# Where the weights' parts stand inside their tiles: 23 products and 24 units of a feed-forward moved by multiples of 8 and 16 bytes

## The chip, the cores and the metric

The kernel runs on one core of one Trainium2 chip. The metric is the device time of one execution in microseconds. A profile shows one execution, engine by engine; TensorE is "PE", its weight loads are "PEld", VectorE is "DVE", ScalarE "ACT", GpSimd "POOL" and SyncE "SP".

## The reference

One layer of a bidirectional encoder over 256 tokens of width 2048, all in float32: an RMSNorm and a combined input projection; windowed grouped-query attention with 12 query and 4 key/value heads beside a Fourier group; an output projection with residual; then the feed-forward, which the change is about, and a last RMSNorm.

```python
def _conv_ffn(h, w_up, dw_w, dw_b, w_down):
    up = h @ w_up
    gate, val = up[..., :D_FF], up[..., D_FF:]
    gate = lax.conv_general_dilated(gate, dw_w, ...) + dw_b
    act = jax.nn.gelu(gate, approximate=False) * val
    return act @ w_down
...
        x = x + _conv_ffn(_rmsnorm(x, norm2_g), w_up, dw_w, dw_b, w_down)
    return _rmsnorm(x, normf_g)
```

D_FF is 5504, or 43 tiles of 128 features.

## The kernel before, in words

**Parts.** Every weight tile of 128 × 2048 is loaded as float32 and split into two float32r parts: ScalarE writes `hi` (a copy rounded to float32r), VectorE writes `lo = w − hi`. A product of two float32 matrices is then three matmuls of parts, hi·hi, hi·lo and lo·hi. `split` (line 157) does this for a unit, `split_product` (line 919) for a down product; both issue their next loads behind the split. `hi` and `lo` each rotate through three buffers of 2176 elements, of which 2048 are used, so a part may start up to 128 elements into its tile. The list `shifts` holds that start, in elements of 4 bytes, for each unit. Before the change it is (hi, lo) = (16, 16) for the first eight units, (0, 16) for the query and key units and for all gate and value units, and (0, 0) for the rest; the down products always take (0, 0). 16 elements are 64 bytes.

**Units.** A gate or value unit is the up-projection to one tile of 128 features. `still_weights` (lines 304 to 311) keeps the weights still: for each of the 16 slices of the width it loads 128 × 128 of `hi` and streams the tokens' two parts past it (512 columns, line 308), then loads 128 × 128 of `lo` and streams the tokens' first part (256 columns, line 309): 32 matmuls in one bank of PSUM. The query and key units of the attention have the same form. `moving_weights` (lines 292 to 302) is the other form, used by the first projections, the output projection and the late part of the down-projection: activations stand still and 512 columns of weights stream past.

**Products.** The down-projection of the first 32 feature tiles is done group by group (four groups of eight tiles). In each group, for each half of the columns (c = 0, 1), seven products of sums of blocks stand for eight block products. `by_parts` (lines 1034 to 1040) does one: for each of four slices a piece of the operand is loaded as weights, and 512 columns of the product's `hi` (lines 1038 and 1039) or `lo` (line 1040) are streamed: 12 matmuls.

**Order.** The order of the work is written out by hand. `ff_items` (line 69) lists the feed-forward: 16 units, then for each group the pattern `"uuu" + "su" * 13 + "s"`, where u is a unit of the next group and s a product of this one, then what is left over. While item n is on TensorE, `ff_step` (line 960) issues the split of item n + 2 to ScalarE and VectorE, beside the post-processing of the items behind. All loads of weights go through SP's queue or, for the two sums that a DMA accumulates, through POOL's.

Of the kernel before, what the change touches and what calls it, by code (L numbers as in the profile page):

```python
# [9 lines left out]
F32R = mybir.dt.float32r  # L10
# [3 lines left out]
P = 128  # L14
# [20 lines left out]
SHIFT = 16  # L35
# [15 lines left out]
for _g in range(NKV):  # L51
# [10 lines left out]
PRODUCTS = [  # L62
    ["P1", "P7", "N5", "N3", "P6", "P2", "N4"], ["P1", "N5", "P7", "N3", "P6", "P2", "N4"]
]
# [4 lines left out]
def ff_items():  # L69


    def ups(tiles):
        return [(kind, j) for j in tiles for kind in ("gate", "val")]

    items = ups(range(8))
    for g in range(N_GROUPS):
        todo = {
            "u": ups(range(8 * g + 8, 8 * g + 16)),
            "s": [("product", g, c, p) for c in range(2) for p in PRODUCTS[c]],
        }  # L80
        items += [todo[c].pop(0) for c in PATTERN]
        assert not any(todo.values())
    items += [("down", 0, c) for c in range(4)] + ups(LAST)
    items += [("down", 1, c) for c in range(4)] + [("last", c) for c in range(4)]
    return items
# [3 lines left out]
def block_kernel(  # L89
# [22 lines left out]
    wp = ctx.enter_context(tc.tile_pool(name="wp", bufs=1))  # L112
# [3 lines left out]
    def f32(ap):  # L116
        return ap.bitcast(F32)
# [7 lines left out]
    shifts = [(SHIFT, SHIFT)] * 8 + [(0, SHIFT)] * 16 + [(0, 0)] * 16  # L125
    n_front = len(units)
    items, up_index = ff_items(), {}
    for n, it in enumerate(items):
        if it[0] == "product":
            continue  # L130
        up_index[n] = len(units)
        if it[0] in ("gate", "val"):
            units.append((w_up[2 * it[1] + (it[0] == "val")], 2048))
            shifts.append((0, SHIFT))
            continue
        elif it[0] == "down":
            units.append((w_down_late[4 * it[1] + it[2]], 2048))
        else:
            units.append((w_down_last[it[1]], 512 * len(LAST)))
        shifts.append((0, 0))  # L140
# [9 lines left out]
    def parts_of(i):  # L150
        halves[i] = tuple(
            wp.tile([P, 2176], F32R, tag=h, name=f"{h}{i}", bufs=3)[:, s : s + 2048]
            for h, s in zip(("hi", "lo"), shifts[i])
        )
        return halves[i]
# [44 lines left out]
    def u_part(k, o, n, m=1):  # L200

        rows = ux[k // 4][:, (k < 4) * U_HEAD :].rearrange("p (k c) -> p k c", k=4)
        return rows[:, k % 4 : k % 4 + m, o : o + n]
# [148 lines left out]
    for k in range(NK):  # L352
        c, q = k // 4, k % 4
        if q == 0:
            hi, lo = (t.rearrange("p (k c) -> p k c", k=4) for t in parts_of(c))
        n = 1 if c < 2 else 2
# [3 lines left out]
        if q % n == 0:  # L360
            w, h = u_part(k, 0, FW, n), hi[:, q : q + n, :]
# [545 lines left out]
    def weights_of(g, c, w):  # L907
        return w_down[(g * 2 + c) * 4 + "abcd".index(w)]

    def ring_load():  # L910
        if ring_next[0] < len(ring):
            key = ring[ring_next[0]]
            ring_next[0] += 1
            ring_tiles[key] = fp.tile([P, 2048], F32, tag="rawd", name="rawd%d%d%s" % key)
            nc.sync.dma_start(ring_tiles[key], weights_of(*key))
# [3 lines left out]
    def split_product(g, c, p):  # L919

        raw = {w: ring_tiles.get((g, c, w)) for w in "abcd"}
        x = ring_tiles["x"]
        src = {"P1": raw["a"], "N3": raw["d"], "P7": raw["b"], "P2": raw["c"]}.get(p, x)
        hi, lo = (
            wp.tile([P, 2176], F32R, tag=h, name=f"{h}_{p}_{g}{c}", bufs=3)[:, 0:2048]
            for h in ("hi", "lo")
        )
        halves["product", g, c, p] = (hi, lo)
        nc.scalar.activation(hi, src, AF.Copy)  # L929
        nc.vector.tensor_tensor(lo, src, f32(hi), ALU.subtract)  # L930
        if p in ("P1", "P7", "N3", "P2"):
            ring_load()
        elif p == "N5":
            nc.gpsimd.dma_start(x, weights_of(g, c, "d"), accum_op=ALU.add)
        elif p == "P6":
            nc.gpsimd.dma_start(x, weights_of(g, c, "c"), accum_op=ALU.add)
        elif p == "N4" and (g, c) != (N_GROUPS - 1, 1):
            pending.append(lambda: first_sums(g + c, 1 - c))

    def first_sums(g, c):  # L940

        a, b = ring_tiles[g, c, "a"], ring_tiles[g, c, "b"]
        x = ring_tiles["x"] = fp.tile([P, 2048], F32, tag="sumw", name=f"sumw{g}{c}", bufs=1)
        nc.vector.tensor_tensor(x, a, b, ALU.add)
        nc.gpsimd.dma_start(b, weights_of(g, c, "d"), accum_op=ALU.add)

    def split_item(n):
        if n >= len(items):
            return
        it = items[n]  # L950
        if n in up_index:
            split(up_index[n])
            if pending:
                pending.pop(0)()
        else:
            while pending:
                pending.pop(0)()
            split_product(*it[1:])
# [159 lines left out]
    for n, it in enumerate(items):  # L1118
# [15 lines left out]
        if it[0] == "product":  # L1134
            kind, g, c, p = it
# [10 lines left out]
        else:  # L1146
            kind, g, c = it
            hi, lo = halves.pop(up_index[n])
# [161 lines left out]
```

## Time and profile before

| | |
|---|---|
| median of 3 runs | 952.45 us (951.67 to 953.35) |
| the profiled execution | 951.68 us |
| its span, first to last instruction | 949.9 us |
| granted TensorE clock | 0.997 of full speed |
| TensorE busy | 940.3 us, 99% of the span, 5085 matmuls |
| VectorE, ScalarE busy | 750.6 us (79%), 534.5 us (56%) |
| mean DMA traffic | 223 GB/s |

A row of a group reads: line, engine, operation, out<-in, shapes, count, then busy time in us, mean ns of one, idle time before. The matmuls are pipelined and the profile models their ends, so two neighbours overlap in it: the distance between their starts is what they cost, and a mean over the undisturbed mean shows that something was lost. A row of the order of time begins with the start and the duration in us.

### The profile page before, as it was taken

To read this page: it belongs to the slowest core of one execution; us is meant where nothing else is said; L and a number is where in the kernel's file an instruction comes from. 1 tells how busy PE (TensorE), PEld (TensorE's weight loads), DVE (VectorE), ACT (ScalarE), POOL (GpSimd) and SP (SyncE) were. 2 spreads that over 40 slices of the span, in tenths; PEclk is the share of its full clock that TensorE was granted. 3 is DMA by queue.
4 is the path that set the end of the run, shared out by engine and by line. 5 is a ranking of instruction groups with operands and counts; after the bars stand their busy time and mean duration, and the time that the engine had idled before them with its cause. 6 is when DMAs were issued, how large, how long until landed. Compare 5 with 4: busy or idle time off the path is not lost.

```text
span 949.9 us, 12779 instructions
## 1 busy us (share of the span) xinstructions
PE 940.3 (99%) x5085; PEld 813.4 (86%) x5085; DVE 750.6 (79%) x935; ACT 534.5 (56%) x646; POOL 43.4 (5%) x58
## 2 busy tenths in 40 slices
PE   9999999999999999999999999999999999999996
PEld 7889998888888888888888888888888888888885
DVE  7758877666676689787898978988779979888775
ACT  7756766455454546556565555665556755553442
POOL 0000000000000000000000000000000000000003
PEclk9999999999999999999999999999999999999998
DMA  9854444446556675978778787877977797776542
GB/s 363 336 187 144 168 142 169 139 172 221 178 177 227 257 224 192 292 234 262 228 257 248 237 304 228 264 250 214 296 253 239 210 296 218 221 244 218 179 134 89
DMA packets 32108, 211.58 MB, mean 223 GB/s; under 512 B 3504, under 2 KB 4016, under 8 KB 7984
## 3 DMA queue, kind: packets, MB, share of 16 engines
q1 hardware_dynamic: 28448, 184.55, 52.4%
q0 software_dynamic: 3600, 26.22, 14.6%
q8 instruction: 40, 0.66, 0.3%
q14 instruction: 20, 0.16, 0.0%
HBM read 208.65 MB, written 2.10 MB: 222 GB/s over the span
## 4 chain that ended last, share of the span: by engine, by line
PE 98%; DVE 1%; DMA 0%; issue 0%; ACT 0%; POOL 0%; POOLq 0%; DVEq 0%; ACTq 0%
PE ps_gate L308 16%; PE ps_val L308 16%; PE ps_gate L309 8%; PE ps_val L309 8%; PE ps_q L308 5%; PE ps_P L1039 3%; PE ps_P L1038 3%; PE ps_P L1040 3%; PE ps_q L309 2%; PE ps_N L1039 2%; PE ps_N L1038 2%; PE ps_a L300 2%; PE ps_a L298 2%; PE ps_N L1040 2%; PE ps_a L299 2%; PE ps_k L308 2%
## 5 line engine op out<-in xcount | busy, mean ns | idle before, releaser
L165 DVE TENSOR_TENSOR lo<-raw,hi 128x2048 fp32r<-128x2048 f32 (+1 forms) x133 | 302.7, 2276 | 54.0 <-ACT hi L164 54.0
L164 ACT ACTIVATE hi<-raw 128x2048 fp32r<-128x2048 f32 (+1 forms) x133 | 253.1, 1903 | 59.7 <-PE ps_l L299 24.7
L308 PE MATMUL ps_gate<-hU,hi 128*128 128x512 f32 x688 | 236.8, 389 | 0.0
L308 PE MATMUL ps_val<-hU,hi 128*128 128x512 f32 x688 | 236.8, 389 | 0.0
L309 PE MATMUL ps_gate<-hU,lo 128*128 128x256 f32 x688 | 190.2, 276 | 0.0
L309 PE MATMUL ps_val<-hU,lo 128*128 128x256 f32 x688 | 190.2, 276 | 0.0
L308 PEld LDWEIGHTS ps_gate<-hU,hi 128*128 128x128 f32 x688 | 129.1, 188 | 27.1
L308 PEld LDWEIGHTS ps_val<-hU,hi 128*128 128x128 f32 x688 | 129.1, 188 | 27.1
L309 PEld LDWEIGHTS ps_gate<-hU,lo 128*128 128x128 f32 x688 | 129.1, 188 | 1.1
L309 PEld LDWEIGHTS ps_val<-hU,lo 128*128 128x128 f32 x688 | 129.1, 188 | 1.1
L820 ACT ACTIVATE ft_g<-ps_gate 128x256 f32<-128x256 f32 x43 | 16.5, 384 | 121.1 <-PE ps_gate L309 121.1
L820 ACT ACTIVATE ft_v<-ps_val 128x256 f32<-128x256 f32 x43 | 16.5, 385 | 89.9 <-PE ps_val L309 89.9
L308 PE MATMUL ps_q<-hT,hi 128*128 128x512 f32 x192 | 66.9, 393 | 0.0
L309 PE MATMUL ps_q<-hT,lo 128*128 128x256 f32 x192 | 53.2, 277 | 0.0
L1039 PE MATMUL ps_P<-hi_P,op_P 128*128 128x512 f32 x128 | 50.2, 392 | 0.0
L1038 PE MATMUL ps_P<-hi_P,op_P 128*128 128x512 f32 x128 | 50.1, 392 | 0.0
L1040 PE MATMUL ps_P<-lo_P,op_P 128*128 128x512 f32 x128 | 49.8, 389 | 0.0
L930 DVE TENSOR_TENSOR lo_N<-sumw,hi_N 128x2048 fp32r<-128x2048 f32 x16 | 36.6, 2290 | 10.1 <-ACT hi_N L929 10.1
L308 PEld LDWEIGHTS ps_q<-hT,hi 128*128 128x128 f32 x192 | 36.1, 188 | 7.2
L822 DVE TENSOR_TENSOR fa_g<-ps_gate,ft_g 128x256 f32<-128x256 f32 x43 | 18.2, 423 | 25.0 <-ACT ft_g L820 25.0
L298 PE MATMUL ps_a<-hi,cat 128*128 128x512 f32 x96 | 37.9, 395 | 0.0
L1039 PE MATMUL ps_N<-hi_N,op_N 128*128 128x512 f32 x96 | 37.6, 392 | 0.0
(332 smaller groups left out, 1608.1 us busy)
## 6 DMA issues: line engine op xcount, KB each, us to landing
raw<-in_w_up SPq DMA_DIRECT2D x86, 1024.0 KB, 5.1
raw<-in_w_in SPq DMA_DIRECT2D x20, 1024.0 KB, 4.9
raw<-in_w_out SPq DMA_DIRECT2D x16, 1024.0 KB, 4.8
sumw<-in_w_down POOLq DMA_DIRECT2D x16, 1024.0 KB, 8.5
raw<-in_w_down_late SPq DMA_DIRECT2D x8, 1024.0 KB, 4.8
raw<-in_w_down_last SPq DMA_DIRECT2D x4, 768.0 KB, 4.3
ux<-in_w_u_x SPq DMA_DIRECT2D x3, 768.0 KB, 9.5
xs<-in_x SPq DMA_DIRECT2D x4, 512.0 KB, 16.2
```

The costliest lines, as they stand in the source:

```text
L164: nc.scalar.activation(hi[:, 0:n], raw[:, 0:n], AF.Copy)
L165: nc.vector.tensor_tensor(lo[:, 0:n], raw[:, 0:n], f32(hi[:, 0:n]), ALU.subtract)
L298: nc.tensor.matmul(ps, ah, wh, start=first and q == q0, stop=False)
L299: nc.tensor.matmul(ps, al, wh, start=False, stop=False)
L300: nc.tensor.matmul(ps, ah, wl, start=False, stop=last and q == q0 + len(kk) - 1)
L308: nc.tensor.matmul(ps, hi[:, s], hk(k), start=k == 0, stop=False)
L309: nc.tensor.matmul(ps[:, 0:S], lo[:, s], hk(k)[:, 0:S], start=False, stop=k == NK - 1)
L820: nc.scalar.activation(tmp, ps[:, S : 2 * S], AF.Copy)
L930: nc.vector.tensor_tensor(lo, src, f32(hi), ALU.subtract)
L1038: nc.tensor.matmul(ps, o[:, 0, p, :], hi[:, s], start=first and p == 0, stop=False)
L1039: nc.tensor.matmul(ps, o[:, 1, p, :], hi[:, s], start=False, stop=False)
L1040: nc.tensor.matmul(ps, o[:, 0, p, :], lo[:, s], start=False, stop=last and p == 3)
```

## The change

Two tables are made before the units are listed. `shift_of` gives each product of groups 0 and 1 a pair of starts: 16 products take (0, 0), (4, 4), ... (60, 60), that is hi and lo in step by 16 bytes each time; four move lo alone, by 4, 60, 16 and 48 elements; two move hi alone, by 4 and 60; two move both, by 2 and 62 elements, which are 8 bytes past a multiple of 16; the last four of the 28 stay at (0, 0). `kind_of` gives the gate or value unit that stands behind a product of groups 2 and 3 a pair from a grid: hi at 0, 4, −4, 8 or −8 elements (the negative ones counted from 64), lo at 16 and the same steps around it. 25 units take one each; the first, (0, 16), is the old place. All other products and units keep their places, and so do the two units behind a product of group 3 for which no pair is left.

```diff
+    shift_of, kind_of = {}, {}
+    todo = [(x, x) for x in range(0, 64, 4)] + [(0, 4), (0, 60), (0, 16), (0, 48)]
+    todo += [(4, 0), (60, 0), (2, 2), (62, 62)]
+    for g in range(2):
+        for c in range(2):
+            for p in PRODUCTS[c]:
+                shift_of[g, c, p] = todo.pop(0) if todo else (0, 0)
+    kinds = [(4 * a % 64, 16 + 4 * b) for a in (0, 1, -1, 2, -2) for b in (0, 1, -1, 2, -2)]
     for n, it in enumerate(items):
...
         if it[0] in ("gate", "val"):
             units.append((w_up[2 * it[1] + (it[0] == "val")], 2048))
-            shifts.append((0, SHIFT))
+            if items[n - 1][0] == "product" and items[n - 1][1] >= 2 and kinds:
+                kind_of[n] = kinds.pop(0)
+            shifts.append(kind_of.get(n, (0, SHIFT)))
             continue
...
         hi, lo = (
-            wp.tile([P, 2176], F32R, tag=h, name=f"{h}_{p}_{g}{c}", bufs=3)[:, 0:2048]
-            for h in ("hi", "lo")
+            wp.tile([P, 2176], F32R, tag=h, name=f"{h}_{p}_{g}{c}", bufs=3)[:, s : s + 2048]
+            for h, s in zip(("hi", "lo"), shift_of.get((g, c, p), (0, 0)))
         )
         halves["product", g, c, p] = (hi, lo)
```

## The prediction

> **What bounds the kernel now.** I read the page first: busy shares, the granted clock, the chain that ended last. Then the waits of TensorE, then the groups by line with shapes kept apart, and last the order of time around single units, because the change moves addresses and nothing else.
>
> ```profile
> PE 940.3 (99%) x5085; PEld 813.4 (86%) x5085; DVE 750.6 (79%) x935; ACT 534.5 (56%) x646; POOL 43.4 (5%) x58
> PEclk9999999999999999999999999999999999999998
> PE 98%; DVE 1%; DMA 0%; issue 0%; ACT 0%; POOL 0%; POOLq 0%; DVEq 0%; ACTq 0%
> ```
>
> TensorE is busy 99% of the span and carries 98% of the chain at a clock that the throttle left alone. The list of TensorE's waits has one line for the whole execution, and it lies at the very start:
>
> ```profile
> PE ps_warm L245 <- POOL ones L237: 1.0, 1, 1.0
> ```
>
> So the feed-forward is a row of matmuls that stand one behind the other, and only what changes the length of a matmul, or makes one wait, can move the time. Here are the groups by line with shapes apart (out<-in, shape, count, then busy us and mean ns of one); the first two are the gate units, then the query and key units, the down products, the output projection and the late down units:
>
> ```profile
> L308 PE MATMUL ps_gate<-hU,hi 128*128 128x512 f32 x688 | 236.8, 389 | 0.0
> L309 PE MATMUL ps_gate<-hU,lo 128*128 128x256 f32 x688 | 190.2, 276 | 0.0
> ...
> L308 PE MATMUL ps_q<-hT,hi 128*128 128x512 f32 x192 | 66.9, 393 | 0.0
> L309 PE MATMUL ps_q<-hT,lo 128*128 128x256 f32 x192 | 53.2, 277 | 0.0
> L1039 PE MATMUL ps_P<-hi_P,op_P 128*128 128x512 f32 x128 | 50.2, 392 | 0.0
> L1038 PE MATMUL ps_P<-hi_P,op_P 128*128 128x512 f32 x128 | 50.1, 392 | 0.0
> L1040 PE MATMUL ps_P<-lo_P,op_P 128*128 128x512 f32 x128 | 49.8, 389 | 0.0
> L298 PE MATMUL ps_a<-hi,cat 128*128 128x512 f32 x96 | 37.9, 395 | 0.0
> ...
> L300 PE MATMUL ps_a<-lo,cat 128*128 128x512 f32 x96 | 37.5, 391 | 0.0
> L299 PE MATMUL ps_a<-hi,cat 128*128 128x512 f32 x96 | 37.3, 389 | 0.0
> ...
> L299 PE MATMUL ps_l<-hi,act 128*128 128x512 f32 x64 | 24.9, 389 | 0.0
> L298 PE MATMUL ps_l<-hi,act 128*128 128x512 f32 x64 | 24.9, 389 | 0.0
> L300 PE MATMUL ps_l<-lo,act 128*128 128x512 f32 x64 | 24.9, 389 | 0.0
> ...
> L308 PE MATMUL ps_k<-hT,hi 128*128 128x512 f32 x64 | 22.7, 396 | 0.0
> ...
> L309 PE MATMUL ps_k<-hT,lo 128*128 128x256 f32 x64 | 18.0, 281 | 0.0
> ```
>
> The reader is to see that one and the same form has several lengths. An undisturbed matmul of 512 columns reads 389 ns and one of 256 columns 276 ns; the key units, built just as the gate units are, read 396 and 281. (The ends are modelled, so 389 is no rate; only the surplus over 389 or 276 is time.) The order of time shows the same as starts of the first matmul of a unit or product and of what follows it:
>
> ```profile
> 107.11 0.39 PE L308 MATMUL ps_k<-hT,hi 128*128 128x512 f32 x1
> 112.72 0.49 PE L662 MATMUL ps_t<-ident,sc 128*128 128x128 f32 x3
> 113.86 0.39 PE L308 MATMUL ps_q<-hT,hi 128*128 128x512 f32 x1
> 119.31 0.28 PE L684 MATMUL ps_o<-pt,v_hi 128*128 128x256 f32 x1
> 340.14 0.39 PE L308 MATMUL ps_val<-hU,hi 128*128 128x512 f32 x1
> 345.58 0.39 PE L308 MATMUL ps_gate<-hU,hi 128*128 128x512 f32 x1
> 370.11 0.39 PE L1038 MATMUL ps_P<-hi_P,op_P 128*128 128x512 f32 x1
> 371.50 0.39 PE L1038 MATMUL ps_P<-hi_P,op_P 128*128 128x512 f32 x1
> 372.86 0.39 PE L308 MATMUL ps_gate<-hU,hi 128*128 128x512 f32 x1
> 378.32 0.39 PE L1038 MATMUL ps_N<-hi_N,op_N 128*128 128x512 f32 x1
> ```
>
> A unit of 32 matmuls takes 345.58 − 340.14 = 5.44 us where units follow one another, 119.31 − 113.86 = 5.45 us in a clean query unit, but 112.72 − 107.11 = 5.61 us in this key unit: it is caught in a slower state, 0.17 us longer from its second matmul to its last. A product's first six matmuls take 371.50 − 370.11 = 1.39 us and its last six 1.36 us: it loses about 0.03 us on its way in and then runs clean. The unit behind a product takes 378.32 − 372.86 = 5.46 us: 0.02 us lost on its way in. So three things can happen after a switch between kinds of work: clean at once, a short run-in, or caught to the end.
>
> **The change part by part.** (1) Nothing is added, removed or reordered: every instruction keeps its engine, shape, order and waits, no DMA moves, and the tiles keep their addresses. Only the start inside the 2176-element tile changes, so 2048 elements still fit at the largest place (62 elements). As counts of work this costs 0.
>
> (2) Products of groups 0 and 1 (28 listed, 23 of them really moved: the first and the last four stay at 0). In 19 hi moves, in 21 lo. The parts are the streamed operand of lines 1038 to 1040. What a product loses today is, by the rows, (392 − 389) × 2 × 4 = 24 ns. No row shows a streamed operand off the 64-byte grid against its partner, since every shift in the kernel now is 0 or 16 elements of 4 bytes. The bounds: if the run-in vanishes, as in the late down units (389 in all three lines), a product gains 24 ns; if all twelve matmuls stall by the 6 ns of the worst line (ps_a L298, 395), it takes 12 × 6 = 72 ns and loses 48 more. I take the nearest row of the same helper order and place (0, 0), the output projection, where pieces enter in many ways: (6 + 0 + 2) × 4 = 32 ns, so +8 ns a product, 23 × 8 ns = +0.2 us.
>
> (3) Units behind a product in groups 2 and 3 (25 listed, 24 moved; the first keeps (0, 16)). Here hi and lo are the stationary operand of lines 308 and 309, loaded beside the matmul before. A moved unit starts from a phase that the trace does not have. The bounds: the run-in vanishes, −0.02 us a unit; or the unit is caught like the key unit, 5.61 − 5.46 = +0.15 us. Which one is nearest? The sixteen query and key units are the only rows where units of this form start from varied phases. All four key units are caught (281 against 276), and the query units' 277 is one fifth of the way from 276 to 281, worth 2.4 of 12 units: together 6.4 of 16, a share of 0.40. An uncaught one loses between 0 and 0.02 us, I take 0.01. So a unit changes by 0.40 × 0.17 + 0.60 × 0.01 − 0.02 = +0.054 us, and 24 of them by +1.3 us.
>
> (4) The neighbours. The unit behind a moved product, and the product behind a moved unit, keep their own places but may enter in another phase. They run in over about five matmuls now whatever came before, so I take 0; both ends lie inside the bounds of (2) and (3), since a caught state ends with the next switch.
>
> (5) The copies that write the parts also meet the new places:
>
> ```profile
> L165 DVE TENSOR_TENSOR lo<-raw,hi 128x2048 fp32r<-128x2048 f32 x130 | 297.4, 2288 | 52.5 <-ACT hi L164 52.5
> L930 DVE TENSOR_TENSOR lo_N<-sumw,hi_N 128x2048 fp32r<-128x2048 f32 x16 | 36.6, 2290 | 10.1 <-ACT hi_N L929 10.1
> L929 ACT ACTIVATE hi_N<-sumw 128x2048 fp32r<-128x2048 f32 x16 | 30.5, 1908 | 0.0
> ...
> 361.90:597.10 235.20, 235.20 (x1266) 203.09 (x1265) 197.49 (x198) 138.42 (x134) 9.60 (x11) 1.00 0.79 248
> 613.50:856.00 242.50, 242.50 (x1298) 209.09 (x1298) 211.13 (x224) 142.14 (x137) 10.21 (x12) 1.00 0.78 244
> ```
>
> The last two rows are the stretches of groups 0 and 1 and of groups 2 and 3 (span, then busy time of PE, PEld, DVE, ACT, POOL). With both parts in step (L930, 0 and 0) or 64 bytes apart (most of L165) the subtraction takes 2290 or 2288 ns, so the place is worth 2 ns there. DVE has 235.20 − 197.49 = 37.7 us free in the first stretch and 31.4 us in the second: the 23 moved subtractions would have to grow by 1.6 us each before VectorE bound the stage, the 24 in the second by 1.3 us. I cost this at 0; what hides it is that TensorE never waits for a part.
>
> The sum is +0.2 + 1.3 = +1.5 us. The profiled execution took 951.68 us (span 949.9), so it would take 953.2; it lies 0.77 us under the median of the runs, 952.45, and against that median I forecast 953.95 us.
>
> The stall itself is where a page speaks against this. The Trainium skill, TensorE: Matmul & The Clock Gate, section "Step-by-step: what each phase is for", says that TensorE reads SBUF through two independent ports, one for the streamed operand and one for the weights. By that rule no place could make the one wait for the other and the sum would be 0. The trace does not bear it out alone: the same form with the same shapes has 276 and 281 ns with nothing waited for, though what the 5 ns are, no row says.
>
> **The rivals.**
> - *Places do not matter.* The stall belongs to the switch of kinds alone, and the moved starts re-enter as before: 0 us, 952.45. For it: clean runs in both the (0, 0) late down units and the (0, 16) gate units, both 389. Against: the key units' 396 and 281 in places that are just the same as the clean units' show a state that a small phase can set. This is also what the two-port rule named above would give.
> - *Slower: the new places catch their units.* A stationary part off the 64-byte grid conflicts in each of its 32 matmuls as in the key units: 24 × 0.15 = 3.6 us; with all products stalled at 6 ns a matmul 23 × 0.048 = 1.1 us more: +4.7 us, 957.15. It passes 0.2% (1.9 us) when about 12 of the 24 units are caught: 12 × 0.15 − 12 × 0.01 and the products' 0.2. For it: four of four key units. Against: the caught units sit in unmoved places, so the catch need not come from the place.
> - *The run-in vanishes.* The new phases enter clean: 24 × 0.02 + 23 × 0.024 = −1.03 us, 951.4. For it: the clean query unit at 5.45 us. Against: it asks for 47 lucky places. It cannot reach −0.2%.
> - *The copies bind.* Starts off 16 or 32 bytes make VectorE's 2.29 us about twice as long: 23 × 2.29 = 52.7 us over 37.7 free would cost 15 us, 967. Against: 2288 and 2290 ns in two different relations of the parts, and an elementwise stream has no reason in these rows to halve its rate.
>
> **How the numbers follow.** The mixture (forecast) has 0.46, places do not matter 0.16, caught (from +1.9 to +4.7) 0.27, the run-in vanishes 0.09, the copies bind 0.02. The range from 951.3 to 957.2 takes in the bounds of (2) and (3), −1.03 and +4.7, on the median. The mixture's own range is +0.7 to +2.5 (between a share of 0.2 and of 0.65 caught), 953.15 to 954.95; a bit more than a quarter of its chance lies over +1.9 us. About 0.2% is what a measurement here can tell from no change. So slower by more than that: 0.27 + 0.02 + 0.46 × 0.28 = 0.42; faster by more than that only through a gain that no row shows, 0.03; within, 0.55.
>
> **What would show it.** In the changed kernel the counts of every group stay. Steps (2) and (3) are seen in the stretches of groups 0 and 1 and of groups 2 and 3: the forecast wants the first 0.2 us and the second 1.3 us longer. In the means, L1038 and L1039 stay near 392; L308 and L309 of gate and val rise by 1.3 us over 1376 pairs, about 1 ns a pair. Single units of 5.6 us among those of 5.46 us behind a product show the catch; a unit well over 5.61 us would show a price that the trace of before does not have. The copies of step (5) must stay at 2288 to 2293 ns, and TensorE's list of waits at one line. The prediction is wrong if moved parts cost more than 5 to 6 ns a matmul (a fetch that the off-grid start adds), if a caught state outlives the unit, or if the run-ins go for good.

## The result and the profile after

The changed kernel takes 956.5 us (median of 3 runs, 956.45 to 956.81) against 952.45 before: a ratio of 1.0049, with an interval of 1.0035 to 1.0062, or +3.3 to +5.9 us. The two profiled executions have spans of 954.7 and 949.9 us, 4.8 us apart, and the traces account for all of it. In this kernel the product's lines 1038 to 1040 have become 1050 to 1052, the unit's 308 and 309 are 320 and 321, and the two subtractions 165 and 930 are 177 and 942. First the page (busy time, and the chain that ended last), then the groups by line with shapes apart:

```profile
PE 945.1 (99%) x5085; PEld 815.2 (85%) x5085; DVE 750.4 (79%) x935; ACT 534.8 (56%) x646; POOL 43.4 (5%) x58
...
PE 98%; DVE 1%; DMA 0%; issue 0%; ACT 0%; POOL 0%; POOLq 0%; DVEq 0%; ACTq 0%
```

```profile
L177 DVE TENSOR_TENSOR lo<-raw,hi 128x2048 fp32r<-128x2048 f32 x130 | 297.3, 2287 | 52.6 <-ACT hi L176 52.6
...
L320 PE MATMUL ps_val<-hU,hi 128*128 128x512 f32 x688 | 238.7, 391 | 0.0
L320 PE MATMUL ps_gate<-hU,hi 128*128 128x512 f32 x688 | 238.5, 391 | 0.0
L321 PE MATMUL ps_gate<-hU,lo 128*128 128x256 f32 x688 | 191.0, 278 | 0.0
L321 PE MATMUL ps_val<-hU,lo 128*128 128x256 f32 x688 | 191.0, 278 | 0.0
...
L1052 PE MATMUL ps_P<-lo_P,op_P 128*128 128x512 f32 x128 | 50.2, 392 | 0.0
...
L942 DVE TENSOR_TENSOR lo_N<-sumw,hi_N 128x2048 fp32r<-128x2048 f32 x16 | 36.6, 2290 | 10.1 <-ACT hi_N L941 10.1
```

The counts are the old ones. VectorE's busy time and its copies have not moved (2287 and 2290 ns), while TensorE's busy time has grown by 4.8 us, which is the whole of the difference. The means of the up-projection have gone from 389 and 276 ns to 391 and 278, and line 1052, the products' `lo`, from 389 to 392.

Where it happened is seen in the order of time. Before, these were the starts of the first product of group 0, of the first product of group 2 and of the last product of group 3; then the same three after:

```profile
361.90 0.39 PE L1038 MATMUL ps_P<-hi_P,op_P 128*128 128x512 f32 x1
...
613.45 0.39 PE L1038 MATMUL ps_P<-hi_P,op_P 128*128 128x512 f32 x1
...
845.91 0.39 PE L1038 MATMUL ps_N<-hi_N,op_N 128*128 128x512 f32 x1
```

```profile
361.86 0.39 PE L1050 MATMUL ps_P<-hi_P,op_P 128*128 128x512 f32 x1
...
615.00 0.39 PE L1050 MATMUL ps_P<-hi_P,op_P 128*128 128x512 f32 x1
...
850.68 0.39 PE L1050 MATMUL ps_N<-hi_N,op_N 128*128 128x512 f32 x1
```

The stretch with the moved products went from 251.55 to 253.14 us (+1.59), the one with the moved units from 232.46 to 235.68 us (+3.22). Together that is 4.81 us, and outside nothing changed.

From here on, "lost" is the distance from the start of a matmul to the start of the next, less the undisturbed distance (512 columns 226.7 ns, 256 columns 113.3 ns, which make 5.44 us for a unit), summed over a product or a unit. By that measure the 4.8 us are:

```
                                            before    after    more
23 moved products (the other 5 as before)    0.70      1.58    +0.88 us   (28 products)
unmoved units behind or between them         0.61      1.33    +0.72
24 moved units (the other 4 as before)       0.61      3.64    +3.03      (27 units behind a product, 1 behind the late down products)
unmoved products of groups 2 and 3           0.70      0.88    +0.18
```

Single places in the changed kernel, by the starts of a product or unit and of what follows it:

```profile
419.38 0.39 PE L1050 MATMUL ps_P<-hi_P,op_P 128*128 128x512 f32 x1
...
422.10 0.39 PE L320 MATMUL ps_gate<-hU,hi 128*128 128x512 f32 x1
...
427.54 0.39 PE L1050 MATMUL ps_N<-hi_N,op_N 128*128 128x512 f32 x1
...
471.79 0.40 PE L320 MATMUL ps_gate<-hU,hi 128*128 128x512 f32 x1
...
477.40 0.40 PE L320 MATMUL ps_val<-hU,hi 128*128 128x512 f32 x1
...
483.00 0.40 PE L320 MATMUL ps_gate<-hU,hi 128*128 128x512 f32 x1
...
488.60 0.40 PE L1050 MATMUL ps_P<-hi_P,op_P 128*128 128x512 f32 x1
...
625.95 0.40 PE L320 MATMUL ps_gate<-hU,hi 128*128 128x512 f32 x1
...
631.63 0.39 PE L1050 MATMUL ps_N<-hi_N,op_N 128*128 128x512 f32 x1
```

The product at (28, 28) takes 2.72 us and the unit behind it 5.44 us: both lose nothing, where a product with its unit lost 47 ns before. After the product at (52, 52) three units that did not move take 5.61, 5.60 and 5.60 us one behind the other: they are caught, and stay so until the next product. The moved unit at (0, 20) takes 5.68 us: it lost 238 ns, where the caught key unit that takes 5.61 us lost 162. (Some query and key units of the trace before are as long, with 243 to 246 ns lost; but 88 or 89 of these stand in front of their second matmul.)

### The profile page after: what moved, and what is told of

Its sections match the earlier page's. It is cut to its first block, busy times and chain, and to the rows that moved or that the text cites. A ratio compares the mean times of both kernels' runs of the same rounds, so it can differ in the third digit from the quotient of the medians.

```text
span 954.7 us, 12779 instructions
## 1 busy us (share of the span) xinstructions
PE 945.1 (99%) x5085; PEld 815.2 (85%) x5085; DVE 750.4 (79%) x935; ACT 534.8 (56%) x646; POOL 43.4 (5%) x58
## 4 chain that ended last, share of the span: by engine, by line
PE 98%; DVE 1%; DMA 0%; issue 0%; ACT 0%; POOL 0%; POOLq 0%; DVEq 0%; ACTq 0%
PE ps_val L320 16%; PE ps_gate L320 16%; PE ps_gate L321 8%; PE ps_val L321 8%; PE ps_q L320 5%; PE ps_P L1050 3%; PE ps_P L1052 3%; PE ps_P L1051 3%; PE ps_N L1050 2%; PE ps_N L1052 2%; PE ps_N L1051 2%; PE ps_q L321 2%; PE ps_a L312 2%; PE ps_a L310 2%; PE ps_a L311 2%; PE ps_k L320 2%
## 5 line engine op out<-in xcount | busy, mean ns | idle before, releaser
L942 DVE TENSOR_TENSOR lo_N<-sumw,hi_N 128x2048 fp32r<-128x2048 f32 x16 | 36.6, 2290 | 10.1 <-ACT hi_N L941 10.1
```

## The experiments

**The two halves alone.** The first run takes the moved units back, the second the moved products.

```diff
# products_only
-    kinds = [(4 * a % 64, 16 + 4 * b) for a in (0, 1, -1, 2, -2) for b in (0, 1, -1, 2, -2)]
+    kinds = []
# units_only
-                shift_of[g, c, p] = todo.pop(0) if todo else (0, 0)
+                shift_of[g, c, p] = (0, 0)
```

> The 23 moved products keep their new places, all units of groups 2 and 3 go back to (0, 16). In the changed kernel's trace the matmuls of the moved products lost 0.88 us more than before and the units that did not move but stand behind or soon after them 0.72 us more. Theory A (the place of the parts sets the loss, one unit at a time, and can leave the next units caught): +1.6 us against before, with the same six unmoved units caught (those behind the products at (48, 48) and (52, 52), the two units that follow without a product between, and two behind products of group 1). Theory B (catching is a matter of a chance entry): other units caught than in the changed kernel, and a sum that differs by more than 0.5 us.

> The products all stay at (0, 0); the 24 units of groups 2 and 3 keep their new places. Theory A: the 3.03 us of the moved units and 0.18 us of the unmoved products behind them, +3.2 us against before; together with the other half the whole 4.8 us. Theory B: the sum of the two halves misses the whole by more than 0.5 us, because the entries differ.

Measured: the products alone 953.32 against 951.75 us, ratio 1.0019 (1.0010 to 1.0028), span 951.3; the units alone 955.3 us, ratio 1.0040 (1.0026 to 1.0053), span 955.2. In matmul time the first lost 1.59 us more than before, the second 3.22 us, and the sum is the 4.81 us of the whole. Each of the 28 products and 28 units behind them lost what it lost in the changed kernel to within 1 ns, and the same unmoved units were caught. (The profiled execution of the second run began its key units at 56.2 us in place of 54.1; these 2.0 us lie ahead of all that was changed, and make its span longer than its matmuls.) So theory A: the same places with the same neighbours gave the same loss in all the traces that have them, which leaves no room for a draw.

**All products at the clean place.**

```diff
-            wp.tile([P, 2176], F32R, tag=h, name=f"{h}_{p}_{g}{c}", bufs=3)[:, 0:2048]
+            wp.tile([P, 2176], F32R, tag=h, name=f"{h}_{p}_{g}{c}", bufs=3)[:, 28:2076]
```

> All 56 products take (28, 28), all units (0, 16). In the changed kernel the one product at (28, 28) ran clean from its first matmul (0 against 25 ns lost) and the unit behind it too (0 against 22). Theory A (the place decides): 56 products lose nothing in place of 25 ns and 56 units behind them nothing in place of 22: -2.6 us against before. Theory B (that product had a lucky entry): between -0.3 and +3 us, with losses that differ from product to product.

Measured: 949.31 against 951.75 us, ratio 0.9973 (0.9962 to 0.9983), span 948.2. This version beats both kernels. The groups by line:

```profile
L308 PE MATMUL ps_gate<-hU,hi 128*128 128x512 f32 x688 | 236.2, 389 | 0.0
...
L1038 PE MATMUL ps_P<-hi_P,op_P 128*128 128x512 f32 x128 | 49.8, 389 | 0.0
L1039 PE MATMUL ps_P<-hi_P,op_P 128*128 128x512 f32 x128 | 49.8, 389 | 0.0
L1040 PE MATMUL ps_P<-lo_P,op_P 128*128 128x512 f32 x128 | 49.8, 389 | 0.0
```

The products' 392, 392 and 389 ns of before are 389 in all three lines. By the starts, all 56 products and all 55 units behind one lost under 1 ns. It is what theory A asked for: −2.6 us by the matmuls and −2.4 us by the medians.

**Relation or place.** Three runs move the weights of the units, the tokens that stream past them, or both, by 32 bytes (8 elements). The tokens' tiles are moved by taking a small tile of 32 bytes from behind them to in front of them, so that every other address stays; the first 24 units, of the attention, are moved with the tokens.

```diff
# w8: the weights of the 86 gate and value units
-            shifts.append((0, SHIFT))
+            shifts.append((8, SHIFT + 8))
# x8: the tokens (and the first 24 units with them); both8: x8 and w8
-    shifts = [(SHIFT, SHIFT)] * 8 + [(0, SHIFT)] * 16 + [(0, 0)] * 16
+    shifts = [(SHIFT + 8, SHIFT + 8)] * 8 + [(8, SHIFT + 8)] * 16 + [(0, 0)] * 16
...
+    ssq1 = base.tile([P, 2, 4], F32, tag="ssq1", name="ssq1")
     for c in range(4):
         t = base.tile([P, 4, 512], F32R, tag=f"hT{c}", name=f"hT{c}")
...
-    ssq1 = base.tile([P, 2, 4], F32, tag="ssq1", name="ssq1")
```

> All 86 gate and value units take (8, 24), which is 32 bytes past their old (0, 16); the tokens that stream past them stay. The one unit at (8, 24) in the changed kernel lost 142 ns over its 32 matmuls, the 24 moved units 126 on average against 22 before. Theory of the relation (what counts is how the standing and the streamed operand lie to each other) and theory of the place (what counts is that a part starts off the 64-byte grid) both say 86 x 110 to 142 ns less the present run-ins (56 x 22 ns): +8 to +11 us.

> The tokens that stream past the units (hT, hU) start 32 bytes further on, and the gate and value units stay at (0, 16); the first 24 units, which belong to the attention, are moved by the same 32 bytes, so that nothing changes between their operands. Theory of the relation: the gate and value units' weights now lie 8 elements ahead of what streams, as in the unit at (56, 8) of the changed kernel (111 ns): 86 x 111 ns less 56 x 22 ns, about +8 us. Theory of the place of the weights: their places did not move, so 0, within 0.3 us of before.

> Tokens and all weights of the units are moved by the same 32 bytes: hT and hU 32 bytes further on, gate and value units at (8, 24), the first 24 units too. Theory of the relation: as before, within 0.3 us, with 389 and 276 ns in the gate units. Theory of the place: both operands are off the 64-byte grid of before, +8 us or more.

(The 126 in the first of these is the rise of the moved units; what they lost was 148 ns on average.) Measured: weights alone 963.47 against 951.93 us, ratio 1.0122 (1.0107 to 1.0137); tokens alone 958.18, ratio 1.0071 (1.0056 to 1.0086); both 952.64, ratio 1.0008 (0.9998 to 1.0017). The groups by line of the three, in that order:

```profile
L308 PE MATMUL ps_val<-hU,hi 128*128 128x512 f32 x688 | 242.0, 393 | 0.0
...
L309 PE MATMUL ps_val<-hU,lo 128*128 128x256 f32 x688 | 192.9, 280 | 0.0
```

```profile
L308 PE MATMUL ps_gate<-hU,hi 128*128 128x512 f32 x688 | 240.7, 391 | 0.0
...
L309 PE MATMUL ps_val<-hU,lo 128*128 128x256 f32 x688 | 192.0, 279 | 0.0
...
L1040 PE MATMUL ps_P<-lo_P,op_P 128*128 128x512 f32 x128 | 49.8, 389 | 0.0
L1039 PE MATMUL ps_P<-hi_P,op_P 128*128 128x512 f32 x128 | 49.8, 389 | 0.0
L1038 PE MATMUL ps_P<-hi_P,op_P 128*128 128x512 f32 x128 | 49.8, 389 | 0.0
```

```profile
L165 DVE TENSOR_TENSOR lo<-raw,hi 128x2048 fp32r<-128x2048 f32 x130 | 297.3, 2287 | 53.1 <-ACT hi L164 53.1
...
L308 PE MATMUL ps_gate<-hU,hi 128*128 128x512 f32 x688 | 236.4, 389 | 0.0
...
L309 PE MATMUL ps_val<-hU,lo 128*128 128x256 f32 x688 | 190.2, 276 | 0.0
...
L1040 PE MATMUL ps_P<-lo_P,op_P 128*128 128x512 f32 x128 | 50.7, 396 | 0.0
L1039 PE MATMUL ps_P<-hi_P,op_P 128*128 128x512 f32 x128 | 50.4, 394 | 0.0
L1038 PE MATMUL ps_P<-hi_P,op_P 128*128 128x512 f32 x128 | 49.8, 389 | 0.0
```

Moving either operand of the units costs 2 to 4 ns a matmul over all 2752 of them (+11.5 us, a little over the +8 to +11 expected, and +6.3 us in place of +8); moving both gives 389 and 276 back. For the units, at this one distance of 32 bytes, the relation of the two operands counts, and not the place of either. With the weights moved a unit lost 133 to 147 ns even in a row of units without a product between: it finds no clean state there. VectorE writes the parts to the same off-grid places in the first and third run; its 2287 ns and the third run's 389 leave the copies out of it.

The last two fences hold something that nobody had expected. In both runs no address of a product changed. Yet in the second the products run clean (389 in all three lines), although every unit between them lost 106 ns or more; and in the third they lose 49 ns each in place of 25. That is the +0.7 us of the third run, which the expected 0.3 did not allow for: 56 × 24 ns = 1.3 us, less 0.3 us each in the query and key units and in the units behind products. A product's loss is set by what it is entered from, too.

**A map of the products' places.** Each of the 56 products has a place of its own; all units stay at (0, 16).

```diff
+    places = [(0, 0), (4, 4), ... (128, 128), (26, 26), (27, 27), (29, 29), (30, 30), (90, 90), (94, 94), (28, 0), ... (28, 28)]
+    shift_of = {it[1:]: places.pop(0) for it in items if it[0] == "product"}
...
-            for h in ("hi", "lo")
+            for h, s in zip(("hi", "lo"), shift_of[g, c, p])
```

> Each of the 56 products takes a place of its own: hi and lo in step at 0, 4, ... 128 elements, six places between (26, 27, 29, 30, 90, 94), and seventeen pairs around (28, 28) with hi and lo apart. All units (0, 16). Theory of the relation with a period: products 64 elements (256 bytes) apart lose the same, so (92, 92) runs clean as (28, 28) did and (64, 64) as (0, 0); the mean over the places is about that of the changed kernel's 23 (62 ns), which makes +2.1 us for the products and some units caught behind them, +2 to +6 us in all. Rival (the losses follow from what was entered from, no map exists): no order in them, and (28, 28) at the end of the list not clean.

Measured: one run, 954.56 us, span 952.8 (+2.9 over before). What the products lost, in ns, worked out from the starts:

```
hi = lo =    0   4   8  12  16  20  24  28  32  36  40  44  48  52  56  60
            25  61  75  40  26  46  91   0  60  76  95  78  69  90  74  89
64 more:    25  61  74  40  27  46  91   0  61  76  95  78  70  91  74  89    (128: 25)
between:    26: 39   27: 71   29: 144   30: 95   90: 52   94: 95
hi, lo:     (28, 0) 62  (0, 28) 48  (28, 24) 87  (28, 32) 37  (24, 28) 73  (32, 28) 56  (28, 92) 0
            (64, 0) 25  (0, 64) 25  (20, 28) 26  (28, 12) 33  (12, 28) 63  (28, 28) 0
```

(Thirteen of the seventeen pairs are shown; the other four lost 0, 71, 27 and 57 ns.) The two rows agree to 1 ns: the loss has a period of 64 elements, 256 bytes. One pair of places 64 apart differs, 26 with 39 ns and 90 with 52, nearly all of it in the first step (2 and 14 ns): the second was entered from a caught unit, the first from one that had run clean. A step of 4 bytes off (28, 28) already costs 71 or 144 ns. There are no safe multiples of 64 bytes: 16 elements lose 26 all along the product, 32 lose 60, 48 lose 69. The catching followed the place as well: behind (48, 48) and (52, 52) the unit lost 157 to 163 ns in every run that had them.

**The same for the units.** All products at (28, 28), and the units behind a product each at a place of its own.

```diff
+    places = [(0, 0), (0, 16), (0, 32), (0, 48), (16, 0), ... (48, 48), (4, 4), ... (60, 44), (52, 36), (52, 20), (36, 52)]
...
-            shifts.append((0, SHIFT))
+            behind_one = items[n - 1][0] == "product" and places
+            shifts.append(places.pop(0) if behind_one else (0, SHIFT))
```

> All products at (28, 28), which run clean, so that each of the 55 units behind one is entered alike; these units take a place each: the sixteen pairs of 0, 16, 32, 48 elements, then hi and lo in step, lo 16 after hi, and lo 48 after hi at the places between, then (52, 36), (52, 20), (36, 52). Theory of the relation with the grid (64 bytes are safe, since the caught units of the changed kernel all lay off it): the sixteen on the grid lose under 30 ns, the rest 100 to 240. Theory of the relation alone (every difference has its own loss, as in the products, where (48, 48) lost 70 and (28, 28) nothing): several of the sixteen lose 100 or more, and one or more places off the grid run clean; (52, 52), which gives both parts the distance that the products have at (28, 28), is the candidate.

Measured: one run, 960.46 us. All sixteen pairs on the 64-byte grid lost 106 to 217 ns, and the 39 others 67 to 212; (52, 52) lost 151. The grid theory falls. (The changed kernel spoke against it already: the six unmoved units caught there lay on the grid, at (0, 16).) Of the places tried with the tokens where they were, (0, 16) is the only one that any run shows clean, and here it lost 160 too: it stood behind a product that had lost 53. For the products at (28, 28) were clean no longer either:

```profile
L1041 PE MATMUL ps_P<-hi_P,op_P 128*128 128x512 f32 x128 | 50.3, 393 | 0.0
L1040 PE MATMUL ps_P<-hi_P,op_P 128*128 128x512 f32 x128 | 50.2, 393 | 0.0
L1042 PE MATMUL ps_P<-lo_P,op_P 128*128 128x512 f32 x128 | 50.2, 392 | 0.0
```

Fifty of the 56 lost 43 to 67 ns, in steps of "−2 4 11" ns over and over. Beside the run with all products at (28, 28) nothing of theirs had moved, only the units around them. So which state a product enters hangs on the unit before it; but not on that unit's loss alone, for in the run with the tokens moved the products ran clean between units that all lost.

**The query and key units**, seven of sixteen of which are caught before and after:

```diff
# beside the products at (28, 28)
-    shifts = [(SHIFT, SHIFT)] * 8 + [(0, SHIFT)] * 16 + [(0, 0)] * 16
+    shifts = [(SHIFT, SHIFT)] * 8 + [(52, 52)] * 16 + [(0, 0)] * 16
```

> All products at (28, 28), and the sixteen query and key units, seven of which are caught in every run so far (about 160 ns each), take (52, 52) in place of (0, 16). If the distance of the clean products is clean in units too, whatever they are entered from: seven times 160 ns and the run-ins of two more go, -1.1 us beside the run with the products at (28, 28), -3.6 us against before. If it is as the moved units of the changed kernel: sixteen units at about 130 ns in place of 1.2 us together, +0.9 us beside that run, -1.6 us against before.

Measured: 950.3 against 951.57 us, ratio 0.9983 (0.9974 to 0.9992), span 948.9, against 948.2 with the products alone. Every one of the sixteen lost 140 to 154 ns from its second matmul on. The distance that is clean in products is not clean in units, as the second case had it.

**The products' standing operands.** They start 32 bytes further on (a tile of 32 bytes ahead of them in the pool), with the streamed weights at 0, 8 and 36 elements. The diff shows the run with 8.

```diff
+            ahead.append(fp.tile([P, 8], F32, tag="ahead", name="ahead", bufs=1))
...
-            wp.tile([P, 2176], F32R, tag=h, name=f"{h}_{p}_{g}{c}", bufs=3)[:, 0:2048]
+            wp.tile([P, 2176], F32R, tag=h, name=f"{h}_{p}_{g}{c}", bufs=3)[:, 8:2056]
```

> The standing operands of all 56 products start 32 bytes (8 elements) further on; the products' weights stay at (0, 0). (The four late down units on those tiles are moved along; the last four are not, which may cost up to 0.4 us at the end in this and the next two runs.) Theory of the relation: a product's weights lie 8 elements behind as those at (56, 56) did, which lost 74 ns and left the next unit clean: 56 x (74 - 25 - 22) = +1.5 us. Theory of the place: the streamed weights did not move, 0.

> Standing operands of the products 32 bytes further on and their weights at (8, 8). Theory of the relation: as before, 25 and 22 ns, 0 (within 0.3 us) in place of the 74 ns of (8, 8) with the operands unmoved. Theory of the place: 56 x (74 - 25) ns and the units behind clean, +1.5 us; that the entry from a unit may shift is a third possibility, as in the run with tokens and weights moved together, where unmoved products went from 25 to 49 ns.

> Standing operands 32 bytes further on, weights of the products at (36, 36), so that they lie as in the clean case (28, 28). Theory of the relation: products and the units behind clean, -2.4 us like the run with all products at (28, 28). Theory of the place: (36, 36) lost 76 ns, and the unit behind it 31: 56 x 60 ns, +3.4 us.

Measured: 963.98 us, ratio 1.0125 (1.0109 to 1.0140); 953.79 us, ratio 1.0019 (1.0009 to 1.0028); 962.11 us, ratio 1.0105 (1.0090 to 1.0120). None of the three has the time that the theory of the relation gave. The middle run's matmuls took 1.5 us more, which is the sum of the theory of the place: its products lost 70 ns each and the units behind them ran clean. The other two lost far more than either theory said. In these kernels the unit's line 308 is 309 and the product's lines 1038 to 1040 are 1044 to 1046. The groups by line of the first run, then of the last:

```profile
L309 PE MATMUL ps_val<-hU,hi 128*128 128x512 f32 x688 | 241.0, 393 | 0.0
```

```profile
L309 PE MATMUL ps_val<-hU,hi 128*128 128x512 f32 x688 | 240.8, 393 | 0.0
...
L1046 PE MATMUL ps_P<-lo_P,op_P 128*128 128x512 f32 x128 | 50.8, 397 | 0.0
L1045 PE MATMUL ps_P<-hi_P,op_P 128*128 128x512 f32 x128 | 50.2, 392 | 0.0
L1044 PE MATMUL ps_P<-hi_P,op_P 128*128 128x512 f32 x128 | 49.7, 388 | 0.0
```

In both, all 55 units behind products, whose operands had not moved, are caught: 153 to 161 ns each. With the six units that follow them without a product between, that is 8.5 and 8.3 us of the 11.7 and 9.8 by which the matmuls grew. What changed for a unit is its border. The weights of the next item are loaded beside the last matmul of this one, as the trace of before shows at the end of a product (first TensorE, then its weight loads):

```profile
380.83 0.39 PE L1040 MATMUL ps_N<-lo_N,op_N 128*128 128x512 f32 x1
...
380.84 0.19 PEld L308 LDWEIGHTS ps_val<-hU,hi 128*128 128x128 f32 x1
```

So the last matmul of a unit now ran beside a load from a moved tile. In the units that ran clean that matmul lost 4 or 5 ns, in all three runs, where it had lost 0 or 1 before: the product is entered late.

The steps of single products tell more than the sums. At (8, 8) the path in is "7 13 2 6 9 −3 4 9 1 6 4" ns, ending in the very steps "4 9 1 6 4" that the product of before begins with; with unmoved operands (8, 8) had ended in steps of "7 4 8". With the weights at 0 the product takes the steps "8 5 8 5" that (56, 56) ended in. At (36, 36), which lies as (28, 28) did, it falls into "4 11 −2" and never comes clean, where (36, 36) with unmoved operands had "7 6 6"; and "4 11 −2" is what the products at (28, 28) did in the map of the units. So in all three runs the relation gave the steps that it had given elsewhere, and the place of the weights did not. What the relation does not tell is where on its path an item is entered and which of its states it takes, and most of the added time hangs on that.

## Why the prediction was right or wrong

The time, 956.5 us, lies in the range (951.3 to 957.2), near its upper end. The chain's reading held: TensorE alone sets the time, and the run-ins and the caught state that the prediction read from the key units are what grew. The forecast of +1.5 us was too small by a factor of three; what happened is the rival "the new places catch their units", at +4.7 us. That its sum lies so near the 4.8 us of the traces is partly luck: it had 3.6 us for the units and 1.1 for the products, which measured 3.03 and 0.88, and nothing for the neighbours, which made the other 0.90.

1. Step (1), nothing but the starts: held.
2. Step (2), products: +0.2 us forecast, +0.88 us measured. The 23 moved products lost 63 ns on average, from 0 to 95, against 25 before, where the step took 32. The upper bound of 72 ns was too low for ten of the 23. The step took the row of the output projection, whose surplus is a run-in that ends; a moved place mostly has no end to it, as the map shows.
3. Step (3), units: +1.3 us forecast, +3.03 us measured, and this is the step that failed. It held catching to be a draw at entry with a share of 0.40, by the key and query units. But those units stand in the one relation that any run shows clean, and seven of the sixteen are caught; the moved units show no clean state. All 24 lost at least 105 ns, 148 on average, and six of them 190 or more, up to 238, over the step's bound of 170. With the weights moved in all 86 units (393 and 280 ns) it is the same in long rows without any entry.
4. Step (4), the neighbours: 0 forecast, +0.90 us measured. The step took a caught state to end with the next switch, and in this kernel the unmoved products behind caught units did run in to clean; but the switch can be two units away, and an unmoved unit behind a moved product can itself be caught: six of them lost 156 to 162 ns. (In the map of the units not even the switch ended the loss.) Seven other unmoved units gained their 22 ns.
5. Step (5), the copies: 0 forecast and 0 measured, 2287 and 2290 ns.
6. "Places do not matter" and the two-port rule beside it fall: 32 bytes in one operand of the units are 11.5 us. The rule of independent ports (the Trainium skill, TensorE: Matmul & The Clock Gate, "Step-by-step: what each phase is for") has no place for it; where the page and the run differ, the run decides.
7. "The run-in vanishes" fell for the change as a whole, but one of its 47 moves does just that, and put on all products it gives −2.4 us.
8. Two of the signs that the prediction named for its being wrong were seen: moved parts that cost more than 5 to 6 ns a matmul (95 ns over the 12 of a product, 238 over the 32 of a unit) and a caught state that outlives the unit.

## What to carry to other kernels

Where TensorE runs without a gap, as here, the start addresses of the two operands can be a tuning parameter of their own: with float32r parts the same groups of matmuls read from 389 to 397 ns by nothing but the places of their operands and of their neighbours'. Judge a place by the whole row of work, since what stands before an item helps to decide its state, and look for places by trying each once in one kernel and reading the starts: the product at (28, 28) was one of 28 in a slower kernel. A change that averages many places tells little by its total time.

## What had not been expected

- The loss of a product depends on the relation of the streamed and the standing operand, with a period of 256 bytes (rows of the map that agree to 1 ns) and a grain of 4 bytes: 29 elements lost 144 ns where 28 lost none.
- The same relation has a clean and a lossy state. The runs show which one a row enters, the same way each time. The last matmul before a switch, beside which the next item's weights are loaded, changes its length with the places of both items; that this sets the state fits the runs but is not shown alone. Why a state holds, and what the 5 ns are inside TensorE or the memory, no run here shows; it stays open. So does a rule that would give the map without running it.
- The start of the kernel varies on its own: in the profiled executions of these kernels the first key unit began between 53.85 and 56.18 us, with nothing changed ahead of it in most. A gain of 2 us is better read from the matmuls of a stage than from one span.
- The caught query and key units, seven of sixteen and about 1.1 us, were not all freed: their one trial, (52, 52), made all sixteen slow. In the two runs with the tokens moved these units kept their relation, yet only four were caught, the four key units not among them, and the sixteen lost 0.3 us less. What else moved for them is not told apart by any run.
